# Hybrid decoder trunk on one core: ScalarE reads a bank ahead of VectorE, and keys and B are turned by VectorE and DRAM

## The chip, the cores and the metric

One core of a Trainium2 chip runs the whole kernel as one program. The metric is device time in microseconds, median of the runs.

## What is computed

Two layers over 512 positions of width 1024. Each layer norms the residual, projects it once to all heads (w_in), feeds four groups of heads, gates each group, projects back (w_out), norms and adds.

```python
hn = rmsnorm(x, pre_g)
proj = hn @ w_in
...
# retention, per head of 128, chunks of 128
q = apply_rope(q)
k = apply_rope(k) * (d ** -0.5)
scores = jnp.einsum('bcnhd,bcmhd->bchnm', qc, kc) * intra.astype(dt)
y_intra = jnp.einsum('bchnm,bcmhe->bcnhe', scores, vc)
kv = jnp.einsum('bcmhd,bcmhe->bchde', kc * zeta.astype(dt)[:, :, None], vc)
...
# state space (SSD), two groups of B and C, chunks of 128
cb = jnp.einsum('bclgn,bcsgn->bclsg', cc, bc)
states = jnp.einsum('bclgn,bclgjp->bcgjpn', bc, xdt * decay_states.astype(dtype)[..., None])
...
# stick-breaking, per block of 128 queries
logits = jnp.einsum('bthd,bshd->bhts', q_blk, k).astype(jnp.float32) * scale
log_1mb = jnp.where(causal, jax.nn.log_sigmoid(-logits), 0.0)
tail = lax.cumsum(log_1mb, axis=3, reverse=True) - log_1mb
w = jnp.where(causal, jnp.exp(log_beta + tail), 0.0)
...
y = jnp.concatenate([y_ret, y_ssd, y_sb, y_mem], axis=-1) @ w_out
return x + rmsnorm(y, post_g)
```

The fourth group (mem) is softmax attention over 256 fixed memory tokens, four heads of 128.

## The kernel before

**Pairs.** fp32 products are made of rounded halves. A `Pair` holds a high half h (rounded) and a low half l = x − h, and `mm3` makes three matmuls of two pairs. `split` (L289 to L291) makes a pair: ScalarE rounds into h (L290), VectorE subtracts for l (L291). Weights arrive by DMA as raw tiles and are split the same way into wh and wl. A projection of 128 output features is a block of 24 matmuls of 128x512 on a PSUM bank called pj; the heads' own products go to banks called mx. There are four banks of each, and a bank is free again when its last reader is done.

**Order of the work.** `layer` runs: stick-breaking's v, four memory heads, four stick-breaking heads, retention's v, four retention heads each followed by a gated memory block, two state-space groups with the gated stick-breaking blocks between, four gated retention blocks, and the output projection. `defer(n, f, ...)` puts the second part of a head n projection blocks later, so that its products are issued among the projections of the next heads. Within that, a scheduler orders the instructions of each engine by its own times, so an edit in one place moves instructions of other places too. Every engine and every DMA queue then works in the order that it was given: SP's queue carries the turned tiles and the decay loads, ScalarE's the raw weights.

**What the change touches.**

- `scaled_pair` (L582 to L586) and `first_chunk` (L588 to L591) serve `sb_head` (L687 to L722). A head's q and k each sit in a pj bank. For q ScalarE writes h, scaled (L584), VectorE l (L585), and ScalarE reads the bank once more for an fp32 copy of the first 128 columns (L590). For k it is `split` and then L590. The four score blocks, of 128, 256, 384 and 512 columns, go through Abs (L709), exponential and logarithm (both L259) on ScalarE, L712, the scan L713 and L715 on VectorE, and a last exponential; L718 masks on GpSimd. Later they are turned by TensorE (L729).
- `ret_head` (L795 to L817): q and k are rotated by VectorE (L769 to L772), the scores of two pairs of chunks go into one mx bank each, which `split` (L805) and a copy (L806) read before GpSimd masks (L808). The first two chunks of k are turned by TensorE (L811) and copied out by ScalarE (L812) into kt; `ret_state`, two blocks later, multiplies kt with v.
- `mem_turn` (L626 to L633): VectorE turns 32 by 32 blocks (L641), four 64 KB writes per tile put them in place in DRAM (L649), and one read brings them back (L651). L663 empties a memory head's bank.
- `ssd_mix` (L986 to L998): the first three chunks of B are turned by TensorE (L996) and copied by ScalarE (L997); `ssd_states` uses them. L959 loads the decays of a group's heads from DRAM, L961 subtracts on VectorE, L962 masks, and L976 turns x on TensorE.

The lines of ret_head that the change rewrites:

```python
kt, b = f[:, 2 * P:], self.mx()
for c in range(2):
    nc.tensor.transpose(b[:, P * c:P * c + P], k.f[:, P * c:P * c + P], self.con("ident", P))
nc.scalar.copy(kt, b[:, :2 * P])
st = self.new(2 * P, F32R)
self.defer(2, self.ret_state, h, v, kt, st)
```

Of the kernel before, what the change touches and what calls it, by code (L numbers as in the profile page):

```python
# [8 lines left out]
F32 = mybir.dt.float32  # L9
# [7 lines left out]
P = 128  # L17
# [136 lines left out]

ROW = 128


# [12 lines left out]
class Builder:  # L172
# [406 lines left out]
            self.mv.append(p)  # L579


    def scaled_pair(self, b, scale):  # L582
        q = Pair(self)
        self.nc.scalar.activation(q.h, b, AF.Copy, scale=scale)  # L584
        self.nc.vector.scalar_tensor_tensor(out=q.l, in0=b, scalar=scale, in1=q.hf, op0=ALU.mult, op1=ALU.subtract)  # L585
        return q  # L586

    def first_chunk(self, b, scale, out):  # L588

        self.nc.scalar.activation(out, b[:, :P], AF.Copy, scale=scale)  # L590
        return out  # L591

    @staticmethod
    def vcols(v, t, h):
# [29 lines left out]
        return o  # L624

    def mem_turn(self, h, w, y):  # L626
        pT = []
        for m in range(2):
            T = self.buf(tag="y")
            for t in range(NT):  # L630
                o = 256 * (t % 2) + P * m
                self.blocks_turned(T, t, w[t // 2][:, o:o + P])
            pT.append(self.through_dram(T))  # L633
        self.defer(4, self.mem_head2, h, pT, y)

    def blocks_turned(self, T, t, x):


        B = 32
        n = T.shape[1] // P  # L640
        self.nc.vector.transpose(v3(T, P // B)[:, :, B * t:B * t + B], v3(x, P // B))  # L641

    def through_dram(self, T, tag="s"):

        B = 32
        d = self.dr.tile([P, SEQ], F32, tag="turned", name=self.name("turned"), bufs=4)[:]
        dd = d.rearrange("(j m) (a t) -> a m j t", m=B, a=P // B)
        for a in range(P // B):
            self.nc.sync.dma_start(dd[a], v3(T[B * a:B * a + B], P // B))  # L649
        x = self.buf(tag="y")  # L650
        self.nc.sync.dma_start(x, d)  # L651
        return x

    def mem_head2(self, h, pT, y):
        pT = [self.pair(x) for x in pT]
# [31 lines left out]
    def sb_head(self, h, v):  # L687
        nc = self.nc
        f = self.buf(3 * P)
        b = self.proj_b()  # L690
        q = self.scaled_pair(b, SCALE)
        q.f = self.first_chunk(b, SCALE, f[:, :P])
        b = self.proj_b()
        k = self.pair(b)
        k.f = self.first_chunk(b, 1.0, f[:, P:2 * P])
        w = [t[:, c] for t, c in self.packed([P * (t + 1) for t in range(NT)], self.buf)]
        run = self.con("run", SEQ)
        for t in range(NT):
# [96 lines left out]
    def ret_head(self, h, v):  # L795
        nc = self.nc
        q = self.rope(self.proj_b())
        k = self.rope(self.proj_b())
        sc, f = Pair(self), self.buf()
        for i in range(2):  # L800
            b, o, fs = self.mx(), 2 * P * i, slice(P * i, P * i + P)
            c, last = slice(o, o + 2 * P), slice(o + P, o + 2 * P)
            self.mm3(b[:, :2 * P], k.h[:, o:o + P], k.l[:, o:o + P], q.h[:, c], q.l[:, c], True, True)
            self.mm(b[:, 2 * P:3 * P], k.f[:, last], q.f[:, last], True, True)
            self.split(b[:, :2 * P], sc.h[:, c], sc.l[:, c], sc.hf[:, c])  # L805
            nc.scalar.copy(f[:, fs], b[:, 2 * P:3 * P])  # L806
            for d in (sc.h[:, o:o + P], sc.l[:, o:o + P], f[:, fs]):
                nc.gpsimd.affine_select(out=d, in_=d, pattern=[[1, P]], compare_op=ALU.is_ge, fill=0.0, base=0, channel_multiplier=-1)  # L808
        kt, b = f[:, 2 * P:], self.mx()
        for c in range(2):  # L810
            nc.tensor.transpose(b[:, P * c:P * c + P], k.f[:, P * c:P * c + P], self.con("ident", P))  # L811
        nc.scalar.copy(kt, b[:, :2 * P])  # L812
        st = self.new(2 * P, F32R)
        self.defer(2, self.ret_state, h, v, kt, st)
        y = self.buf(tag="y")
        self.defer(4, self.ret_head2, h, v, sc, f, st, q, y)
        return y  # L817
# [116 lines left out]
    def ssd_group(self, l, g, ysb):  # L934

        X = {"l": l, "g": g}
        self.ssd_decay(X)
        X["x"] = [self.conv(self.proj_b(), 2 * g + i) for i in range(2)]
        self.defer(2, self.ssd_values, X)
        self.gated(("sb", 2 * g), ysb[2 * g])  # L940
        X["b"] = self.conv(self.proj_b(), 4 + g)
        X["c"] = self.conv(self.proj_b(), 6 + g)
        self.defer(3, self.ssd_mix, X)
        self.gated(("sb", 2 * g + 1), ysb[2 * g + 1])
        X["y"] = [self.buf(tag="y"), self.buf(tag="y")]
        X["z"] = [self.gate(self.proj_b()) for _ in range(2)]
        self.defer(1, self.ssd_states, X)
        self.defer(3, self.ssd_out, X, 0)
        self.defer(3, self.ssd_out, X, 1)
        self.defer(5, self.ssd_var, X)  # L950
        self.defer(9, self.ssd_norm, X)
# [34 lines left out]
    def ssd_mix(self, X):  # L986
# [4 lines left out]
            self.mm(cb[:, s], bT[:, s], cT[:, s], True, True)  # L991
        for a in X["A"]:
            nc.vector.tensor_tensor(out=a, in0=a, in1=cb, op=ALU.mult)
        bt, b = self.buf(), self.mx()
        for c in range(NT - 1):
            nc.tensor.transpose(b[:, P * c:P * c + P], bT[:, P * c:P * c + P], self.con("ident", P))  # L996
        nc.scalar.copy(bt[:, :384], b[:, :384])  # L997
        X["bt"] = bt  # L998

    def ssd_states(self, X):  # L1000

# [311 lines left out]
```

## Time and profile before

| | |
|---|---|
| median of 3 runs | 939.14 us (938.91 to 940.09) |
| profiled execution | 938.47 us |
| its span, first to last instruction | 936.7 us |
| mean granted TensorE clock | 0.998 |
| matmul instructions (PE) | 4775 |
| busy: PE, PEld, DVE, ACT, POOL | 99%, 84%, 71%, 48%, 11% |

PE is TensorE, PEld its weight load, DVE VectorE, ACT ScalarE, POOL GpSimd, SP the queue that issues most transfers. A timeline row gives start, duration, engine, line, operation, output<-input, how many instructions of the kind stand in a row, and in brackets the idle time before them with what ended it. Times count from the start of the span.

### The profile page before, as it was taken

The page shows a single profiled execution, that of the slowest core. Times are in us where ns is not written, and L with a number is a line of the kernel's source. Part 1 is how long each engine was busy: PE and PEld are TensorE (multiplying, and loading weights), DVE is VectorE, ACT ScalarE, POOL GpSimd, SP SyncE. Part 2 cuts the span into 40 slices and gives each one's busy share as a digit, 9 for nine tenths or more (in the row PEclk, how much of TensorE's full clock was granted, in tenths as well). Part 3 has the DMA queues.
Part 4 walks back from the last instruction along what each step waited for, and adds up shares of the span by engine and source line. Part 5 has one row for each costly group of instructions (what it writes and reads, how often), then busy time and mean ns, then how long its engine had stood idle before and what let it go on. Part 6 is the DMA issues. An engine that isn't in the chain of part 4 may idle for free.

```text
span 936.7 us, 12791 instructions
## 1 busy us (share of the span) xinstructions
PE 925.5 (99%) x4775; PEld 784.3 (84%) x4775; DVE 667.3 (71%) x1109; ACT 451.6 (48%) x861; POOL 103.3 (11%) x168
## 2 busy tenths in 40 slices
PE   9999999999999999999999999999999999999997
PEld 8998878888888888888899887888888888888885
DVE  6946687767778886844587467878676989687343
ACT  7733585643354442733465337665343644336341
POOL 1200011100031110100050000101000411102001
PEclk9999999999999999999999999999999999999999
DMA  9544530412423423344345265112223252323502
GB/s 325 209 152 125 182 117 1 135 45 91 135 67 136 136 91 124 135 146 157 118 177 181 92 185 174 46 46 90 90 91 135 69 175 96 124 73 105 205 12 90
DMA packets 38910, 114.35 MB, mean 122 GB/s; under 512 B 5824, under 2 KB 14272, under 8 KB 29760
## 3 DMA queue, kind: packets, MB, share of 16 engines
q10 hardware_dynamic: 10224, 73.44, 22.6%
q1 hardware_dynamic: 28624, 40.11, 13.4%
q8 instruction: 37, 0.61, 0.3%
q14 instruction: 25, 0.20, 0.1%
HBM read 105.02 MB, written 8.48 MB: 121 GB/s over the span
## 4 chain that ended last, share of the span: by engine, by line
PE 96%; ACT 1%; DVE 1%; DMA 0%; issue 0%; DVEq 0%; SPq 0%; ACTq 0%; POOLq 0%; POOL 0%
PE pj L282 72%; PE mx L282 22%; PE mx L729 1%; PE mx L476 1%; DMA mem<-memT 0%; DVE s L713 0%; PE mx L976 0%; ACT s L709 0%; ACT wh L290 0%; DVE s L291 0%; PE mx L811 0%; DVE s L712 0%; DVE s L585 0%; ACT s L520 0%; PE mx L996 0%
## 5 line engine op out<-in xcount | busy, mean ns | idle before, releaser
L282 PE MATMUL pj<-hTh,wh 128*128 128x512 f32 x704 | 277.7, 394 | 2.5 <-ACT s L590 2.5
L291 DVE TENSOR_TENSOR wl<-raw,wh 128x1024 fp32r<-128x1024 f32 (+2 forms) x156 | 184.6, 1187 | 130.5 <-ACT wh L290 129.7
L282 PE MATMUL pj<-hTh,wl 128*128 128x512 f32 x704 | 275.6, 392 | 0.0
L282 PE MATMUL pj<-hTl,wh 128*128 128x512 f32 x704 | 275.1, 391 | 0.0
L290 ACT CAST wh<-raw 128x1024 fp32r<-128x1024 f32 (+2 forms) x156 | 158.6, 1020 | 229.5 <-PE pj L282 208.2
L282 PEld LDWEIGHTS pj<-hTh,wh 128*128 128x128 f32 x704 | 132.3, 188 | 30.3 <-ACT s L590 3.3
L282 PEld LDWEIGHTS pj<-hTh,wl 128*128 128x128 f32 x704 | 132.3, 188 | 27.1
L282 PEld LDWEIGHTS pj<-hTl,wh 128*128 128x128 f32 x704 | 132.3, 188 | 26.3
L282 PE MATMUL pj<-wh,s 128*128 128x512 f32 x320 | 97.7, 391 | 0.0
L282 PE MATMUL mx<-wh,s 128*128 128x512 f32 x256 | 79.2, 389 | 0.0
L282 PE MATMUL mx<-s,s 128*128 128x256 f32 (+3 forms) x528 | 77.7, 307 | 0.0
L291 DVE TENSOR_TENSOR s<-y,s 128x512 fp32r<-128x512 f32 x80 | 51.9, 684 | 27.5 <-ACT s L290 21.8
L282 PEld LDWEIGHTS mx<-s,s 128*128 128x128 f32 (+1 forms) x528 | 65.4, 177 | 7.2 <-issue 2.3
L282 PEld LDWEIGHTS pj<-wh,s 128*128 128x128 f32 x320 | 59.7, 188 | 12.4
L290 ACT CAST s<-y 128x512 fp32r<-128x512 f32 x80 | 46.5, 618 | 28.6 <-PE mx L282 22.0
L282 PE MATMUL pj<-wl,s 128*128 128x512 f32 x160 | 60.2, 389 | 0.0
L282 PEld LDWEIGHTS mx<-wh,s 128*128 128x128 f32 x256 | 48.1, 188 | 10.0
L259 ACT ACTIVATE s<-s 128x384 f32<-128x384 f32 (+3 forms) x96 | 41.4, 479 | 20.8 <-DVE s L715 20.7
L282 PE MATMUL mx<-wl,s 128*128 128x512 f32 x128 | 49.6, 389 | 0.0
L718 POOL TENSOR_SCALAR_AFFINE_SELECT s<-s 128x128 f32<-128x128 f32 x32 | 17.8, 565 | 280.5 <-ACT s L259 280.5
L282 PE MATMUL pj<-wl,hTh 128*128 128x256 f32 (+2 forms) x144 | 48.1, 334 | 0.0
L282 PE MATMUL pj<-wh,hTl 128*128 128x256 f32 (+2 forms) x144 | 48.0, 334 | 0.0
(185 smaller groups left out, 1273.0 us busy)
## 6 DMA issues: line engine op xcount, KB each, us to landing
raw<-wts ACTq DMA_DIRECT2D x69, 1024.0 KB, 4.8
s<-x SPq DMA_DIRECT2D x24, 256.0 KB, 3.8
turned<-y SPq DMA_DIRECT2D x64, 64.0 KB, 2.3
y<-turned SPq DMA_DIRECT2D x16, 256.0 KB, 2.8
s<-acs SPq DMA_DIRECT2D x16, 256.0 KB, 7.2
r<-row SPq DMA_DIRECT2D x12, 256.0 KB, 4.1
raw<-wts SPq DMA_DIRECT2D x4, 512.0 KB, 6.6
raw<-wts SPq DMA_DIRECT2D x2, 1024.0 KB, 6.4
```

The source lines that it names most:

```text
L259: i = self.nc.scalar.activation(out, in_, func, **k)
L282: return self.nc.tensor.matmul(out, lhsT, rhs, start=start, stop=stop)
L290: self.nc.scalar.copy(h, src)
L291: self.nc.vector.tensor_sub(l, src, hf)
L476: x = self.nc.tensor.transpose(b[:, P * j:P * j + P], hn[i][:, P * j:P * j + P], self.con("ident", P))
L718: nc.gpsimd.affine_select(out=d, in_=d, pattern=[[-1, P]], compare_op=ALU.is_gt, fill=0.0, base=0, channel_multiplier=1)
L729: nc.tensor.transpose(b[:, P * t:P * t + P], w[t][:, P * j:P * j + P], self.con("ident", P))
```

## The change

- `scaled_pair` makes the high half, then ScalarE's first-chunk copy, then VectorE's low half, for q and now for k too (scale 1.0, a subtraction). `first_chunk` is gone.
- In `ret_head` ScalarE copies the high half of the scores and the fp32 chunk, and VectorE subtracts last.
- The first two chunks of a retention head's keys, and the first three of B, are turned by `columns_turned`: one VectorE transpose of 32 by 32 blocks, four writes to DRAM in runs of 128 bytes, and one read back. `ret_state` comes four blocks later rather than two. B's turn is issued at B's convolution, and its buffer taken there.
- `mem_turn` turns 256 columns with one instruction, with the same DRAM traffic.

```diff
-    def scaled_pair(self, b, scale):
+    def scaled_pair(self, b, scale, f):
         q = Pair(self)
         self.nc.scalar.activation(q.h, b, AF.Copy, scale=scale)
-        self.nc.vector.scalar_tensor_tensor(out=q.l, in0=b, scalar=scale, in1=q.hf, op0=ALU.mult, op1=ALU.subtract)
+        self.nc.scalar.activation(f, b[:, :P], AF.Copy, scale=scale)
+        if scale == 1.0:
+            self.nc.vector.tensor_sub(q.l, b, q.hf)
+        else:
+            self.nc.vector.scalar_tensor_tensor(out=q.l, in0=b, scalar=scale, in1=q.hf, op0=ALU.mult, op1=ALU.subtract)
+        q.f = f
         return q
...
     def mem_turn(self, h, w, y):
...
-            for t in range(NT):
-                o = 256 * (t % 2) + P * m
-                self.blocks_turned(T, t, w[t // 2][:, o:o + P])
-            pT.append(self.through_dram(T))
+            for i in range(2):
+                x = w[i].rearrange("p (t m j b) -> p m t j b", t=2, m=2, b=BLK)[:, m]
+                nc.vector.transpose(T.rearrange("p (j t b) -> p t j b", t=NT, b=BLK)[:, 2 * i:2 * i + 2], x)
+            d = self.turned_rows(P, SEQ)
+            dd = d.rearrange("(j m) (a t) -> a m j t", m=BLK, a=P // BLK)
+            pT.append(self.through_dram(T, dd, d, self.buf(tag="y")))
...
+    def columns_turned(self, tiles, out):
+        n = sum(x.shape[1] for x in tiles[:1])
+        d = self.turned_rows(n, P * len(tiles))
+        for k, x in enumerate(tiles):
+            T = self.buf(n, TT)
+            self.nc.vector.transpose(T, x)
+            dd = d[:, P * k:P * k + P].rearrange("(b t) (a f) -> a t b f", t=BLK, a=P // BLK)
+            for a in range(P // BLK):
+                self.nc.sync.dma_start(dd[a], v3(T[BLK * a:BLK * a + BLK], n // BLK))
+        r = d.rearrange("(c p) f -> p c f", p=P)
+        c = 0
+        for o in out:
+            k = o.shape[1] // (P * len(tiles))
+            self.nc.sync.dma_start(v3(o, k), r[:, c:c + k])
+            c += k
...
     def sb_head(self, h, v):
...
-        q = self.scaled_pair(b, SCALE)
-        q.f = self.first_chunk(b, SCALE, f[:, :P])
+        q = self.scaled_pair(b, SCALE, f[:, :P])
         b = self.proj_b()
-        k = self.pair(b)
-        k.f = self.first_chunk(b, 1.0, f[:, P:2 * P])
+        k = self.scaled_pair(b, 1.0, f[:, P:2 * P])
...
     def ret_head(self, h, v):
...
-            self.split(b[:, :2 * P], sc.h[:, c], sc.l[:, c], sc.hf[:, c])
+            nc.scalar.copy(sc.h[:, c], b[:, :2 * P])
             nc.scalar.copy(f[:, fs], b[:, 2 * P:3 * P])
+            nc.vector.tensor_sub(sc.l[:, c], b[:, :2 * P], sc.hf[:, c])
...
-        kt, b = f[:, 2 * P:], self.mx()
-        for c in range(2):
-            nc.tensor.transpose(b[:, P * c:P * c + P], k.f[:, P * c:P * c + P], self.con("ident", P))
-        nc.scalar.copy(kt, b[:, :2 * P])
+        kt = f[:, 2 * P:]
+        self.columns_turned([k.f[:, :2 * P]], [kt])
         st = self.new(2 * P, F32R)
-        self.defer(2, self.ret_state, h, v, kt, st)
+        self.defer(4, self.ret_state, h, v, kt, st)
...
         X["b"] = self.conv(self.proj_b(), 4 + g)
+        X["bt"] = self.buf()[:, :3 * P]
+        self.columns_turned([X["b"][:, :3 * P]], [X["bt"]])
         X["c"] = self.conv(self.proj_b(), 6 + g)
...
-        bt, b = self.buf(), self.mx()
-        for c in range(NT - 1):
-            nc.tensor.transpose(b[:, P * c:P * c + P], bT[:, P * c:P * c + P], self.con("ident", P))
-        nc.scalar.copy(bt[:, :384], b[:, :384])
-        X["bt"] = bt
```

Over the program this takes 28 transposes off TensorE (16 of L811, 12 of L996) and 12 copies off ScalarE, and adds 60 transfers on SP (48 writes, 12 reads). VectorE's transposes go from 64 to 44.

Three places show how instructions move; the names end in running numbers, and pj, mx, s, y, wh, wl are the tiles told of above.

VectorE in layer 1, from a split of a turned memory tile (y178) to the low half of head 1's q in bank pj246; s233 holds the 128 and 256 wide score blocks of head 0, s234 the 384, s235 the 512. Before:

```order
L291 TENSOR_TENSOR s243_1335<-y178_1010,s242_1334 128x512
L712 SCALAR_TENSOR_TENSOR s233_1283<-mx236_1286,s233_1283 128x128
L712 SCALAR_TENSOR_TENSOR s233_1283<-mx237_1296,s233_1283 128x256
L713 SCALAR_TENSOR_TENSOR s233_1283<-consts_72,s233_1283 128x128
L713 SCALAR_TENSOR_TENSOR s233_1283<-consts_72,s233_1283 128x256
L712 SCALAR_TENSOR_TENSOR s234_1284<-mx238_1308,s234_1284 128x384
L715 TENSOR_TENSOR s233_1283<-mx236_1286,s233_1283 128x128
L715 TENSOR_TENSOR s233_1283<-mx237_1296,s233_1283 128x256
L291 TENSOR_TENSOR s245_1339<-y181_1022,s244_1338 128x512
L713 SCALAR_TENSOR_TENSOR s234_1284<-consts_72,s234_1284 128x384
L712 SCALAR_TENSOR_TENSOR s235_1285<-mx239_1320,s235_1285 128x512
L585 SCALAR_TENSOR_TENSOR s251_1374<-pj246_1342,s250_1373 128x512
```

and now:

```order
L726 SCALAR_TENSOR_TENSOR s233_1267<-mx236_1270,s233_1267 128x128
L727 SCALAR_TENSOR_TENSOR s233_1267<-consts_72,s233_1267 128x128
L729 TENSOR_TENSOR s233_1267<-mx236_1270,s233_1267 128x128
L293 TENSOR_TENSOR s243_1319<-y178_1000,s242_1318 128x512
L726 SCALAR_TENSOR_TENSOR s233_1267<-mx237_1280,s233_1267 128x256
L727 SCALAR_TENSOR_TENSOR s233_1267<-consts_72,s233_1267 128x256
L729 TENSOR_TENSOR s233_1267<-mx237_1280,s233_1267 128x256
L293 TENSOR_TENSOR s245_1323<-y181_1010,s244_1322 128x512
L726 SCALAR_TENSOR_TENSOR s234_1268<-mx238_1292,s234_1268 128x384
L726 SCALAR_TENSOR_TENSOR s235_1269<-mx239_1304,s235_1269 128x512
L727 SCALAR_TENSOR_TENSOR s234_1268<-consts_72,s234_1268 128x384
L592 SCALAR_TENSOR_TENSOR s251_1358<-pj246_1326,s250_1357 128x512
```

The same eleven operations stand ahead of the low half of q; the narrowest block's three now come ahead of the split of y178.

TensorE in layer 1, where stick-breaking's last head meets retention's v (pj338); L729 and now L743 turn the weights of head 0. Before:

```order
L729 MATMUL mx288_1537<-consts_72,s235_1285 128x128
L729 MATMUL mx289_1544<-consts_72,s233_1283 128x128
L729 MATMUL mx289_1544<-consts_72,s234_1284 128x128
L729 MATMUL mx289_1544<-consts_72,s235_1285 128x128
L282 MATMUL pj338_1818<-wh258_1419,hTh_79 128x512
```

and now, where the "..." stands for 18 more matmuls of pj338:

```order
L743 MATMUL mx288_1521<-consts_72,s235_1269 128x128
L284 MATMUL pj338_1802<-wh258_1403,hTh_79 128x512
...
L284 MATMUL pj338_1802<-wl310_1669,hTh_79 128x512
L743 MATMUL mx289_1528<-consts_72,s233_1267 128x128
L743 MATMUL mx289_1528<-consts_72,s234_1268 128x128
```

The turns into bank mx289 moved behind 20 matmuls of the retention projection.

SP in layer 1, at the end of retention: the decay loads of the first state-space group. Before, they follow the memory heads' last turned tile:

```order
L649 DMA turned216_1198<-y215_1193 32x4x128 x4
L651 DMA y217_1203<-turned216_1198 128x512
L959 DMA s514_2737<-acs134_722 128x512
L959 DMA s515_2744<-acs134_722 128x512
```

and now they follow the turned keys of retention's heads 2 and 3:

```order
L662 DMA turned468_2480<-y469_2481 32x8x32 x4
L667 DMA s465_2457<-turned468_2480 128x2x128
L662 DMA turned500_2654<-y501_2655 32x8x32 x4
L667 DMA s497_2631<-turned500_2654 128x2x128
L974 DMA s518_2737<-acs134_722 128x512
L974 DMA s519_2744<-acs134_722 128x512
```

Four writes and a read per retention head now stand ahead of the decay loads.

## Rows read from the trace of the kernel before

**Rows 1.** The page, busy times by engine and DMA packets.

```profile
PE 925.5 (99%) x4775; PEld 784.3 (84%) x4775; DVE 667.3 (71%) x1109; ACT 451.6 (48%) x861; POOL 103.3 (11%) x168
...
DMA packets 38910, 114.35 MB, mean 122 GB/s; under 512 B 5824, under 2 KB 14272, under 8 KB 29760
```

**Rows 2.** The page, chain that ended last, by engine.

```profile
PE 96%; ACT 1%; DVE 1%; DMA 0%; issue 0%; DVEq 0%; SPq 0%; ACTq 0%; POOLq 0%; POOL 0%
```

**Rows 3.** TensorE's waits: line waited for, us in total, times, longest.

```profile
PE pj L282 <- ACT s L590: 2.5, 2, 1.2
...
PE mx L729 <- ACT y L663: 0.7, 2, 0.3
```

**Rows 4.** Groups by line: count | busy us, mean ns | idle before.

```profile
L641 DVE STREAM_TRANSPOSE y<-s 128x128 f32<-128x128 f32 x64 | 14.4, 278 | 0.0
...
L811 PE MATMUL mx<-consts,s 128*128 128x128 f32 x16 | 3.0, 272 | 0.0
...
L996 PE MATMUL mx<-consts,s 128*128 128x128 f32 x12 | 2.0, 273 | 0.0
```

**Rows 5.** The chain in order of time: start, us, what, two pieces.

```profile
306.00 0.33 PE mx L996 x3
...
386.23 40.13 PE pj L282 x177
```

**Rows 6.** Timeline 114 to 126 us, ScalarE, VectorE and TensorE.

```profile
115.10 0.93 ACT L709 ACTIVATE s<-mx 128x128 f32<-128x128 f32 x3
115.91 0.63 ACT L259 ACTIVATE s<-s 128x128 f32<-128x128 f32 x2
...
117.97 0.69 DVE L291 TENSOR_TENSOR s<-y,s 128x512 fp32r<-128x512 f32 x1 [1.51 <-ACT s L290]
...
120.31 0.61 ACT L584 ACTIVATE s<-pj 128x512 fp32r<-128x512 f32 x1
...
123.16 0.67 DVE L585 SCALAR_TENSOR_TENSOR s<-pj,s 128x512 fp32r<-128x512 f32 x1
...
124.19 0.50 PE L282 MATMUL pj<-hTh,wh 128*128 128x512 f32 x1 [1.23 <-ACT s L590]
```

**Rows 7.** Timeline 137 to 141 us, TensorE and VectorE.

```profile
138.43 0.60 PE L729 MATMUL mx<-consts,s 128*128 128x128 f32 x4
...
138.78 0.67 DVE L585 SCALAR_TENSOR_TENSOR s<-pj,s 128x512 fp32r<-128x512 f32 x1
...
139.36 0.52 PE L729 MATMUL mx<-consts,s 128*128 128x128 f32 x3 [0.33 <-ACT y L663]
...
139.81 0.19 PEld L282 LDWEIGHTS pj<-wh,hTh 128*128 128x128 f32 x1 [0.18 <-ACT s L590]
```

**Rows 8.** Timeline 240 to 275 us, SP, VectorE and TensorE.

```profile
245.52 1.99 SPq L959 DMA_DIRECT2D s<-acs  x4
...
258.37 0.69 DVE L772 TENSOR_TENSOR s<-s,s 128x512 f32<-128x512 f32 x1
...
265.03 0.38 PE L811 MATMUL mx<-consts,s 128*128 128x128 f32 x2
...
273.01 1.01 DVE L961 TENSOR_TENSOR s<-s,t 128x512 f32<-128x512 f32 x1
```

**Rows 9.** Timeline 111 to 116 us, SP's issues for a turned memory tile.

```profile
111.85 1.77 SPq L649 DMA_DIRECT2D turned<-y  x4
...
115.06 0.34 SPq L651 DMA_DIRECT2D y<-turned  x1
```

**Rows 10.** DMA issues: count, KB each, median us from issue to landing.

```profile
turned<-y SPq DMA_DIRECT2D x64, 64.0 KB, 2.3
y<-turned SPq DMA_DIRECT2D x16, 256.0 KB, 2.8
s<-acs SPq DMA_DIRECT2D x16, 256.0 KB, 7.2
...
t<-r SPq DMA_DIRECT2D x12, 2.0 KB, 1.7
```

More of the change, by code (lines that the diff above doesn't have):

```diff
@@ L153, in shape_constants @@
     return c
+BLK = 32
+TT = "y"
 ROW = 128
@@ L579, in mem_v2 @@
             self.mv.append(p)
-    def scaled_pair(self, b, scale):
+    def scaled_pair(self, b, scale, f):
         q = Pair(self)
         self.nc.scalar.activation(q.h, b, AF.Copy, scale=scale)
-        self.nc.vector.scalar_tensor_tensor(out=q.l, in0=b, scalar=scale, in1=q.hf, op0=ALU.mult, op1=ALU.subtract)
-        return q
-    def first_chunk(self, b, scale, out):
-        self.nc.scalar.activation(out, b[:, :P], AF.Copy, scale=scale)
-        return out
+        self.nc.scalar.activation(f, b[:, :P], AF.Copy, scale=scale)
[4 more added lines that the diff above has]
+        q.f = f
+        return q
     @staticmethod
@@ L626, in mem_turn @@
     def mem_turn(self, h, w, y):
+        nc = self.nc
         pT = []
@@ L629, in mem_turn @@
             T = self.buf(tag="y")
-            for t in range(NT):
-                o = 256 * (t % 2) + P * m
-                self.blocks_turned(T, t, w[t // 2][:, o:o + P])
-            pT.append(self.through_dram(T))
-        self.defer(4, self.mem_head2, h, pT, y)
[L636 to L652, printed above, removed]
+            for i in range(2):
+                x = w[i].rearrange("p (t m j b) -> p m t j b", t=2, m=2, b=BLK)[:, m]
+                nc.vector.transpose(T.rearrange("p (j t b) -> p t j b", t=NT, b=BLK)[:, 2 * i:2 * i + 2], x)
@@ new lines, in mem_turn, with turned_rows, through_dram @@
+            d = self.turned_rows(P, SEQ)
+            dd = d.rearrange("(j m) (a t) -> a m j t", m=BLK, a=P // BLK)
+            pT.append(self.through_dram(T, dd, d, self.buf(tag="y")))
+        self.defer(4, self.mem_head2, h, pT, y)
+    def turned_rows(self, n, m):
+        return self.dr.tile([n, m], F32, tag=f"turned{n}", name=self.name("turned"), bufs=4)[:]
+    def through_dram(self, T, dst, src, out):
+        n = dst.shape[2]
+        for a in range(P // BLK):
+            self.nc.sync.dma_start(dst[a], v3(T[BLK * a:BLK * a + BLK], n))
+        self.nc.sync.dma_start(out, src)
+        return out
@@ new lines, in columns_turned @@
+    def columns_turned(self, tiles, out):
[5 more added lines that the diff above has]
+            dd = d[:, P * k:P * k + P].rearrange("(b t) (a f) -> a t b f", t=BLK, a=P // BLK)
+            for a in range(P // BLK):
+                self.nc.sync.dma_start(dd[a], v3(T[BLK * a:BLK * a + BLK], n // BLK))
[5 more added lines that the diff above has]
+            c += k
```

## The prediction

> **What bounds the kernel.** I began with the page's busy times: TensorE is busy for 925.5 of 936.7 us, VectorE for 71%, ScalarE for 48% [rows 1]. The chain that ended last says the same from the other side: 96% of it is TensorE [rows 2]. So an edit can gain in two ways only: it takes a matmul off TensorE, or it closes a gap in front of one. The granted clock was 0.998, the 2.4 GHz level, over the whole span, so nothing is to be won or lost there.
>
> For the gaps I read TensorE's waits [rows 3]. There are four kinds in all, and the two that matter stand there: line 590 (2.5 us, 2 times, one per layer) and line 663 (0.7 us, 2 times); the change bears on both. The other two, on GpSimd's line 194 and ScalarE's line 520, belong to parts that it leaves alone. Last I read the timeline around both gaps in layer 1 [rows 6, 7]; layer 2 repeats them 460 us later. The sum is made against the profiled execution, 938.47 us; the median of the runs shown is 939.14, that is 0.67 more, and I add that at the end.
>
> **Turns taken off TensorE.** The 16 transposes of line 811 and the 12 of line 996 go [rows 4]. The page's 272 ns is the length of one, not its price, since matmuls overlap. The price is the pitch, which the chain in order of time shows: three of line 996 take 0.33 us there [rows 5], 0.11 us each, and line 811's have the same form. So 28 cost 3.08 us. These stand on the path with no gap in front of them; this term is the safest. The eight copies of line 812 and four of line 997 on ScalarE go as well; TensorE waits for neither, so I count nothing for them.
>
> The row shows a turn at 0.11 us, on an engine that has no free time. The Trainium skill, VectorE: DVE Perf Modes, section Rules for kernel authors, recommends TensorE for a 128 by 128 transpose where PSUM will do as its destination, because VectorE turns 32 by 32 blocks only. By that rule the 28 would be better left, and the sum would lose its first term; the row and the 99% speak against it here.
>
> **What VectorE takes over.** Eight turns of 128x256 and four of 128x384 come, and the memory heads' 64 turns of 128x128 become 32 of twice the size. One of the old takes 278 ns [rows 4]; a new one of 256 columns lies between 0.28 us (only a fixed cost) and 0.56 us (in proportion), one of 384 between 0.28 and 0.83. I take the proportion: at most 7.8 us more on VectorE, less what the memory heads save, on an engine with 269 us idle. The key turn is put ahead of the key's low half, for which the scores wait; TensorE's waits name no half of a key, so the half has some cover there, and I cost half a microsecond at nothing. If that cover were gone, the scores would start half a microsecond late, eight times.
>
> **The turned keys' way through DRAM.** Four writes and a read per head, on SP. The nearest rows are the memory heads' own: from the first of four writes issued to the read issued 3.21 us (111.85 to 115.06) [rows 9], the read lands 2.8 us later [rows 10], so 6.0 us. The new writes carry half the bytes in runs of 128 bytes, 256 runs each. I bound their landing by 1.7 us (the 2 KB writes t<-r, the smallest there) and twice the old 2.3, 4.6 us [rows 10], so the trip by 5.4 and 8.3 us. Head 3's keys are complete at 259.06 [rows 8]; its scores are done when line 811 starts, at 265.03 [rows 8], and the order puts some 8 us of projection between them and the state product, at about 273. That is 13.9 us for a trip of 6; the other heads have a whole head's period, 20 us. Cost: nothing. B of the state space has two projection blocks of 5.4 us more before its use, and costs nothing either.
>
> **The gap on line 590.** In the old order ScalarE rounds q at 120.31, VectorE makes its low part at 123.16, and only then does ScalarE copy the first chunk; until that has read the bank, head 3's q can't start, and TensorE idles 1.23 us [rows 6]. Its last product would have let it start at 124.19 − 1.23 = 122.96. In the new order the copy follows the rounding at once, so ScalarE is out by about 121.3, and VectorE's low part releases the bank. When does it end? The same eleven operations stand ahead of it since the weights' low half, but the order is another: the 128-wide block's three come first, ahead of the split of y. In the old run VectorE idled 1.51 us before that split, to 117.97 [rows 6]. The block's logarithm is now ScalarE's sixth operation after the weight cast, ready near 116.8 (three Abs and two exponentials end at 115.91 + 0.63 = 116.54 [rows 6], a logarithm like one of these adds 0.3). So about 1.0 us of VectorE's work moves into that gap and the low part ends near 123.83 − 1.0 = 122.8 (the eleven took 123.16 − 117.97 = 5.19 us, under half a microsecond each; the three of the narrowest block come to about 1.0). Bounds: if nothing fits, it ends at 123.83 and 0.87 us of the gap stay; at best none does. I take 0.08 left, the end that the order of the rows is nearest to: 1.15 gained, twice, **2.3 us**.
>
> **The gap on line 663.** At 139.36 three transposes wait 0.33 us for a PSUM bank that line 663 empties; then the first retention block waits another 0.18 us for line 590 [rows 7]. In the new order 20 matmuls of that block (4.5 us at 0.227 [rows 5]) stand ahead of the three transposes, so the wait on line 663 is covered. The block itself then wants VectorE's low part at 138.43 + 0.44 = 138.87; it ended at 138.78 + 0.67 = 139.45 [rows 7], and an order changed in the same way brings it 1.0 forward, to about 138.5. Bounds: none to 0.55 gained per layer (0.33 + 0.18, and the first matmul's longer 0.50). I take 0.45, twice: **0.9 us**.
>
> The retention scores' new order (both copies on ScalarE, then the subtraction) has one waiter that the order shows, GpSimd's masking; TensorE's waits name neither. I cost it at nothing.
>
> **Sum:** 3.08 + 2.3 + 0.9 = 6.28. 938.47 − 6.28 = 932.19; with 0.67, **932.9 us**.
>
> **Rivals.**
> 1. The gaps change hands only. The eleven operations could end as late as before, VectorE's low part then holding the bank where ScalarE's copy did. For it: all eleven are still there, and both gaps lie at one engine's pace. Against it: the 1.51 us hole [rows 6]. With 0.87 left twice and nothing gained at the second gap, 3.08 + 0.72 = 3.8 are gained: 935.3; with both gaps as they were, 936.1.
> 2. SP's queue takes it back. SP works in order, and the decay loads of line 959, issued at 245.52 [rows 8], now stand behind head 3's key read, which waits for four writes. They can't go before about 262.5; the four take 2 us to issue and the median lands 7.2 us after its issue [rows 8, 10], so the last lands at about 272 by the old times, where VectorE wants it at 273.01 [rows 8]. Late by 0 to 2 us if they land slower than that median, VectorE then makes the state space's convolution late, for whose transposes TensorE waits with some 0.8 us in hand. Price 0 to 2 us per layer, so up to 4: 934 to 936.9.
> 3. The other side: the key's trip is long. If head 3's trip takes more than the 13.9 us in hand, TensorE stops in front of its state product, with gated projections queued behind it. The gain is eaten at (6.28 + 1.9) / 2 = 4.1 us beyond, a trip of 18 us, and the time is then over 941. That needs the writes to land 12 us later than the old ones; for it speaks that 14,336 packets of 128 bytes are added to 38,910, against it that the smallest writes landed in 1.7 us [rows 1, 10]. The Trainium skill, DMA: Bandwidth & Descriptors, section Specifications, has transfers reach full rate from 512 bytes only; by that rule the 128-byte runs are where this case would come from, and no row here shows them in such a number.
>
> **Chances.** A difference of 0.2%, 1.9 us, is about what a measurement can tell here. The forecast (both gaps mostly closed, no new wait over a microsecond) 0.55; the first rival 0.17; the second 0.20; the third 0.03; and 0.05 for a wait on another engine that no row points to, half of it past 941. The first rival and 0.14 of the second stay under 937.3; in the other 0.06 the decay loads take longer than their median all four, and the time falls within 0.2%. So faster has 0.86, within 0.2% 0.08, slower 0.06. Low end: every gap closed gives 3.08, the 2.5 + 0.7 of the waits [rows 3] and twice the 0.18 at 139.81 [rows 7], 6.6; with a run at the lower edge (0.23 under the median) that is 932.3, and I leave 1.1 below it for the matmuls that run long after a gap (0.50 for 0.39 [rows 6]) and for stops shorter than the view names: 931.2. High end: the second rival's worst, 936.9.
>
> **What would show it.** No row of lines 811 or 996 on TensorE, and 28 fewer matmuls; line 590's or 592's wait under 0.3 us each; no wait on line 663's successor before the first retention block; the first-chunk copy directly behind the rounding on ScalarE. The key writes landing within 5 us. It is wrong if the profile shows a VectorE low part ending later than 123.3 in head 1, a wait of TensorE on the key read, or a new wait in front of the state space's transposes.

## The result, and the profile after

The changed kernel takes 933.95 us (median of 6 runs, 932.8 to 935.38) where the kernel before took 939.29 (median of 6, 938.91 to 940.09): the ratio is 0.9941, with a 95% interval of 0.993 to 0.9952. Its profiled execution took 932.86 us with a span of 931.1, 5.6 us under the span before. One run each of three kernels below had a granted clock of 0.75 or 0.85 and took 1021 to 1157 us; the ratios leave these runs out, and the medians move by 0.2 us at most without them.

TensorE's busy time and the chain of the changed kernel, from its page:

```profile
PE 922.4 (99%) x4747; PEld 781.7 (84%) x4747; DVE 672.1 (72%) x1089; ACT 444.0 (48%) x849; POOL 92.2 (10%) x168
...
PE 94%; DVE 2%; ACT 2%; DMA 1%; issue 0%; DVEq 0%; SPq 0%; ACTq 0%; POOLq 0%; POOL 0%
```

Against [rows 1] 28 matmuls and 3.1 us of TensorE are gone, and VectorE has 4.8 us more. TensorE's waits in the changed kernel:

```profile
PE mx L284 <- POOL b L196: 1.2, 1, 1.2
PE pj L284 <- DVE s L592: 1.0, 2, 0.5
PE pj L284 <- ACT s L522: 0.3, 1, 0.3
```

Against [rows 3], the wait on line 663 is gone. The one on line 590 has changed hands and is less than half: where ScalarE's copy released the bank after 1.2 us, VectorE's low half now does after 0.5. The timeline of the changed kernel around this place, VectorE, ScalarE and TensorE, answers to [rows 6]:

```profile
117.03 0.29 DVE L726 SCALAR_TENSOR_TENSOR s<-mx,s 128x128 f32<-128x128 f32 x1 [0.41 <-ACT s L261]
...
118.03 0.69 DVE L293 TENSOR_TENSOR s<-y,s 128x512 fp32r<-128x512 f32 x1
118.76 0.42 DVE L726 SCALAR_TENSOR_TENSOR s<-mx,s 128x256 f32<-128x256 f32 x1
...
119.22 0.69 DVE L727 TENSOR_TENSOR_SCAN s<-consts,s 128x256 f32<-128x256 f32 x1
...
119.94 0.42 DVE L729 TENSOR_TENSOR s<-mx,s 128x256 f32<-128x256 f32 x1
120.28 0.68 DVE L293 TENSOR_TENSOR s<-y,s 128x512 fp32r<-128x512 f32 x1
...
121.27 0.28 ACT L588 ACTIVATE s<-pj 128x128 f32<-128x128 f32 x1
...
122.95 0.66 DVE L592 SCALAR_TENSOR_TENSOR s<-pj,s 128x512 fp32r<-128x512 f32 x1
...
123.66 0.50 PE L284 MATMUL pj<-hTh,wh 128*128 128x512 f32 x1 [0.52 <-DVE s L592]
```

ScalarE has left the bank at 121.55 (forecast: 121.3); the low half ends at 123.61, 0.8 later than forecast, of which 0.18 is this run's later start. At the second place the low half ends at 138.50, and the first retention block starts right behind it, with no wait for the memory bank ahead of it; compare [rows 7]:

```profile
137.84 0.66 DVE L592 SCALAR_TENSOR_TENSOR s<-pj,s 128x512 fp32r<-128x512 f32 x1
137.87 0.60 PE L743 MATMUL mx<-consts,s 128*128 128x128 f32 x4
...
138.55 0.50 PE L284 MATMUL pj<-wh,hTh 128*128 128x512 f32 x1
```

SP's issues for head 3's keys and the decay loads behind them, against [rows 8, 9]:

```profile
251.98 1.79 SPq L662 DMA_DIRECT2D turned<-y  x4
255.73 0.38 SPq L667 DMA_DIRECT2D s<-turned  x1
256.21 1.83 SPq L974 DMA_DIRECT2D s<-acs  x4
```

The first write was issued at 251.98 and the read landed at 257.87, 5.9 us later; the other three trips of the layer took 7.1, 5.0 and 7.7 us, those of layer 2 5.3, 5.2, 8.4 and 6.0, and B's four 6.7 to 7.8. No wait of TensorE names a key or B.

**How the profiles are compared.** The first 22 us of a run, where the inputs arrive, differ by over 3 us from one execution to the next (last section). So where a profile is set against another below, the time counts from TensorE's first turn of the normed input (line 476 before, 478 after, some 22 us into the span) to the end of the span: 936.74 − 22.18 = 914.56 before, 931.14 − 22.36 = 908.78 after, 5.78 less.

### The profile page after: what moved, and what is told of

The parts are those of the page before. It is cut to its first block, busy times and chain, and to the rows that moved or that the text cites. A ratio compares the mean times of both kernels' runs of the same rounds, so it can differ in the third digit from the quotient of the medians.

```text
span 931.1 us, 12813 instructions
## 1 busy us (share of the span) xinstructions
PE 922.4 (99%) x4747; PEld 781.7 (84%) x4747; DVE 672.1 (72%) x1089; ACT 444.0 (48%) x849; POOL 92.2 (10%) x168
## 2 busy tenths in 40 slices
DMA packets 57790, 118.03 MB, mean 127 GB/s; under 512 B 21120, under 2 KB 33152, under 8 KB 48640
## 4 chain that ended last, share of the span: by engine, by line
PE 94%; DVE 2%; ACT 2%; DMA 1%; issue 0%; DVEq 0%; SPq 0%; ACTq 0%; POOLq 0%; POOL 0%
PE pj L284 71%; PE mx L284 21%; PE mx L743 1%; PE mx L478 1%; DVE s L727 1%; DVE s L726 1%; ACT wh L292 1%; DMA mem<-memT 1%; ACT s L261 0%; PE mx L991 0%; ACT s L723 0%; DVE s L293 0%; DVE wl L293 0%; DVE s L592 0%; ACT s L292 0%
## 5 line engine op out<-in xcount | busy, mean ns | idle before, releaser
L284 PE MATMUL mx<-s,s 128*128 128x256 f32 (+4 forms) x528 | 81.1, 307 | 0.0
L261 ACT ACTIVATE s<-s 128x128 f32<-128x128 f32 (+3 forms) x96 | 41.3, 471 | 23.3 <-DVE s L729 23.1
L284 PE MATMUL pj<-wh,hTh 128*128 128x256 f32 (+2 forms) x144 | 48.3, 336 | 0.2
```

Of the source, the lines that this page charges most:

```text
L261: i = self.nc.scalar.activation(out, in_, func, **k)
L284: return self.nc.tensor.matmul(out, lhsT, rhs, start=start, stop=stop)
```

## The experiments

**The two halves of the change, alone.** First the changed kernel once more.

> The changed kernel once more, beside the others of this call. Theory (28 turns at 0.109 us off TensorE, and gaps in front of TensorE that shrank from 4.5 to 2.3 us): about 933.9, 5.3 under the kernel before. Rival (SP's longer queue and the small writes give some of it back, by an amount that varies from run to run): the same median, with runs that spread over 2 us or more where the kernel before spreads over 1.2, and a profile of a slower run that shows a wait for a DMA which the first profile does not have.

It took 934.0 us, ratio 0.9939 (0.9925 to 0.9952), the same as the first time. The four runs that the ratio uses lie within 0.7 us of each other, where the rival had a spread over 2; the six of the result lie within 2.6, so the spread itself is not settled. Whether SP's queue takes a part is left to the last run of this section.

Then the order of reads alone (`scaled_pair` with its calls, and the scores), all turns as before:

```diff
-        q = self.scaled_pair(b, SCALE)
-        q.f = self.first_chunk(b, SCALE, f[:, :P])
+        q = self.scaled_pair(b, SCALE, f[:, :P])
...
             nc.scalar.copy(f[:, fs], b[:, 2 * P:3 * P])
+            nc.vector.tensor_sub(sc.l[:, c], b[:, :2 * P], sc.hf[:, c])
```

> Only the order of reads: q, k and retention scores read by ScalarE first, by VectorE last; all turns as before. Theory: the gaps alone shrink, 2 x (1.50 - 0.79) + 2 x (0.72 - 0.35) = 2.2 us: about 937.1. Rival (the order of reads gives nothing by itself, the gaps shrank because the turns left VectorE and ScalarE in another order): 939.3, with waits on the low half of q of 1.2 us each.

Measured: 936.91 us, ratio 0.9975 (0.9966 to 0.9985); 912.11 us from the first turn, 2.45 less than before. TensorE waits 0.3 us at line 592 twice. The theory holds, and the size.

The other half, the turns of keys, B and memory weights, with all reads as before:

```diff
+        self.columns_turned([k.f[:, :2 * P]], [kt])
...
-        self.defer(2, self.ret_state, h, v, kt, st)
+        self.defer(4, self.ret_state, h, v, kt, st)
...
-                self.blocks_turned(T, t, w[t // 2][:, o:o + P])
+                nc.vector.transpose(T.rearrange("p (j t b) -> p t j b", t=NT, b=BLK)[:, 2 * i:2 * i + 2], x)
```

> Only the turns: retention keys, B and the memory weights as in the change; q, k and scores read as before. Theory: 28 x 0.109 = 3.05 us off TensorE and nothing given back, and both gaps of the kernel before stay (line 590's successor 1.2 us twice): about 936.2. Rival (the trip through DRAM or VectorE's added turns cost TensorE something): 937 or more, with a new wait in TensorE's list.

Measured: 937.0 us, ratio 0.9975 (0.9965 to 0.9985); 912.21 from the first turn, 2.35 less and not 3.05. Of the 2.35, 0.33 lie behind the last matmul (told below at keys and B alone), so TensorE's part is 2.02, 1.0 short of the theory. A new wait stands in TensorE's list, as the rival had it, but not on a transfer:

```profile
PE pj L284 <- ACT s L592: 1.9, 2, 1.0
PE mx L284 <- DVE s L730: 1.3, 2, 0.7
...
PE mx L744 <- ACT y L678: 0.7, 2, 0.3
```

It is VectorE's last step of a score block in stick-breaking, a part that the turns don't touch. So the order of instructions there is what to look at for the missing 1.0 us; the next run settles it. The two halves gain 4.8 us alone and 5.78 together: 1.0 us hangs on their meeting.

**Which turn costs it.** Memory weights alone:

```diff
-            for t in range(NT):
-                o = 256 * (t % 2) + P * m
-                self.blocks_turned(T, t, w[t // 2][:, o:o + P])
+            for i in range(2):
+                x = w[i].rearrange("p (t m j b) -> p m t j b", t=2, m=2, b=BLK)[:, m]
+                nc.vector.transpose(T.rearrange("p (j t b) -> p t j b", t=NT, b=BLK)[:, 2 * i:2 * i + 2], x)
```

> Only the memory weights' turn in half as many instructions of 256 columns; all else as in the kernel before. Theory (in the run with the turns alone it was this edit that put VectorE's three 128, 256 and 384 wide blocks side by side, and that made the gaps at the first two heads 2.15 us where they were 1.50): no matmul goes and the gaps grow by 0.65 twice: about 940.8. Rival (the edit moves nothing that counts, and the trip through DRAM of keys and B made those gaps): 939.4.

Measured: 940.9 us, as forecast, ratio 1.0012 (1.0004 to 1.0021); 915.85 from the first turn, 1.29 more than before, with the same wait on line 730 (1.3 us, 2 times) as in the run with all turns. VectorE's timeline of this run:

```profile
119.60 1.08 DVE L727 SCALAR_TENSOR_TENSOR s<-mx,s 128x128 f32<-128x128 f32 x3
120.60 1.85 DVE L728 TENSOR_TENSOR_SCAN s<-consts,s 128x128 f32<-128x128 f32 x3
122.36 0.67 DVE L293 TENSOR_TENSOR s<-y,s 128x512 fp32r<-128x512 f32 x1
```

Three blocks of 128, 256 and 384 columns go through each step side by side, and the split of y starts at 122.36 behind all three scans. Behind it comes the last step of the narrowest block, line 730, for which TensorE's next product waits: TensorE stops for 0.66 us until 123.29, and for 0.95 until 125.89. Fewer instructions on VectorE made this kernel slower, through the order that the scheduler made of the rest.

Keys and B alone, memory weights and reads as before:

```diff
+        self.columns_turned([k.f[:, :2 * P]], [kt])
...
-        self.defer(2, self.ret_state, h, v, kt, st)
+        self.defer(4, self.ret_state, h, v, kt, st)
...
+        X["bt"] = self.buf()[:, :3 * P]
+        self.columns_turned([X["b"][:, :3 * P]], [X["bt"]])
```

> Only keys and B turned by VectorE and DRAM; memory weights and all reads as in the kernel before. Theory: VectorE's order in stick-breaking stays as it was before, both gaps keep their 4.47 us, and 28 x 0.109 us go: about 936.4. Rival (the trip through DRAM costs about half a microsecond, which is what the run with all turns fell short of 3.05): 937 or more, with a wait of TensorE on a key, on B or on the decays.

Measured: 936.05 us, ratio 0.9961 (0.9949 to 0.9974); 911.16 from the first turn, 3.40 less. 0.32 of that lies behind the last matmul (6.73 us from its start to the end before, 6.42 here and 6.41 in the changed kernel), so 3.08 are TensorE's, against 3.05 forecast. The waits on lines 590 and 663 are back at 2.5 and 0.7. The rival falls: the trip through DRAM costs TensorE nothing, and no wait of TensorE in this run names a key, B or the decays.

Retention scores alone:

```diff
-            self.split(b[:, :2 * P], sc.h[:, c], sc.l[:, c], sc.hf[:, c])
+            nc.scalar.copy(sc.h[:, c], b[:, :2 * P])
             nc.scalar.copy(f[:, fs], b[:, 2 * P:3 * P])
+            nc.vector.tensor_sub(sc.l[:, c], b[:, :2 * P], sc.hf[:, c])
```

> Only the retention scores' order of reads (both ScalarE copies first, VectorE's subtraction last); all else as in the kernel before. Theory (TensorE waits for none of these reads): the same as before, 939.3, within 0.5. Rival (part of the 2.5 us that the order of reads gained came from here): 938.5 or less.

Measured: 939.12 us, ratio 0.9998 (0.9988 to 1.0008); 914.57 from the first turn. Nothing, as forecast.

**What is left of the gaps.** If VectorE's low half, behind eleven operations, now holds the bank, then a kernel in which ScalarE alone reads it has no gap:

```diff
+    def wide_pair(self, b, scale):
+        q, x = Pair(self), self.buf()
+        self.nc.scalar.activation(q.h, b, AF.Copy, scale=scale)
+        self.nc.scalar.activation(x, b, AF.Copy, scale=scale)
+        self.nc.vector.tensor_sub(q.l, x, q.hf)
+        q.f = x[:, :P]
+        return q
...
-        q = self.scaled_pair(b, SCALE, f[:, :P])
+        q = self.wide_pair(b, SCALE)
```

> The change, with q's fp32 copy 512 columns wide instead of 128, so that VectorE makes the low half from SBUF and ScalarE alone frees the bank. Theory (what is left of the gaps, 0.79 + 0.35 us per layer, is VectorE's low half behind eleven other operations): both gaps close, 2.3 us less than the change: about 931.6. Rival (ScalarE's longer copy delays exponentials and heads by as much, or something else stands ready behind VectorE): 933 to 935, with a wait of the same places on ScalarE.

Measured: 930.9 us, ratio to the kernel before 0.9912 (0.9899 to 0.9926), 3.1 under the change; 906.60 from the first turn, 2.18 under it. ScalarE's rows and TensorE's at the same place of this run:

```profile
120.98 0.61 ACT L600 ACTIVATE s<-pj 128x512 f32<-128x512 f32 x1
...
122.53 0.71 DVE L601 TENSOR_TENSOR s<-s,s 128x512 fp32r<-128x512 f32 x1
...
122.69 0.39 PE L284 MATMUL pj<-hTh,wh 128*128 128x512 f32 x1
```

VectorE's low half starts at 122.53, counted from the first turn 0.1 us earlier than in the change, and ends at 123.24; TensorE starts at 122.69 without a wait. That the low half's place held the bank in the change is thereby shown. The 0.33 us longer copy on ScalarE costs nothing.

**The key's trip and SP's queue.** The change with the turned keys sent through DRAM once more:

```diff
-        self.columns_turned([k.f[:, :2 * P]], [kt])
+        way = self.buf(2 * P, TT)
+        self.columns_turned([k.f[:, :2 * P]], [way])
+        d = self.dr.tile([P, 2 * P], F32, tag="again", name=self.name("again"), bufs=4)[:]
+        nc.sync.dma_start(d, way)
+        nc.sync.dma_start(kt, d)
```

> The change, with the turned keys sent through DRAM a second time, a plain write of 128 KB and a read back, so that SP carries 16 transfers more and a key is late by one more round trip of about 5 us. Theory (13.9 us in hand for head 3 and 20 for the others, 6 used): no change, 933.9. Rival (SP's queue is what the change has used up: decay loads behind the key read come late, and the state space's transposes wait): 935 or more, with a wait of TensorE on VectorE or on a transfer near 270 us.

Measured: 936.06 us, ratio 0.9959 (0.9947 to 0.9972), 2 us over the change: the theory's number is missed. The five runs reach from 934.36 to 937.09, and the profiled one is the slowest. From the first turn it is 3.3 us over the change, in two places of layer 1. About 1.6 of these go at 44 us, ahead of every key, where TensorE waits for a weight that came late:

```profile
44.61 0.51 PE L284 MATMUL pj<-wh,hTh 128*128 128x256 f32 x2 [1.36 <-ACT wh L292]
```

The other 1.7 are the second trip's. TensorE waits for no key. It waits for the state space's sums at 319 us, and VectorE's timeline of this run shows why:

```profile
310.90 0.69 DVE L980 TENSOR_TENSOR s<-s,t 128x512 f32<-128x512 f32 x1 [4.11 <-DMA s<-acs]
311.51 2.47 DVE L1012 TENSOR_TENSOR s<-s,mx 128x512 f32<-128x512 f32 x4
```

The first decay of the second group (L980) now stands ahead of four products of the first (L1012); in the change the four come first. VectorE works in order, so it waited 4.11 us for a load with ready work behind it. The kernel that took the decay loads off SP tells which it was:

```diff
-            nc.sync.dma_start(v3(a, 4), S["rows"][0, r:r + 4].unsqueeze(0).to_broadcast([P, 4, P]))
+            nc.gpsimd.dma_start(v3(a, 4), S["rows"][0, r:r + 4].unsqueeze(0).to_broadcast([P, 4, P]))
...
-            nc.sync.dma_start(v3(E[64 * j:64 * j + 64], 4), S["rows"][1, r:r + 4].unsqueeze(0).to_broadcast([64, 4, P]))
+            nc.gpsimd.dma_start(v3(E[64 * j:64 * j + 64], 4), S["rows"][1, r:r + 4].unsqueeze(0).to_broadcast([64, 4, P]))
```

> The run with the keys' second trip, decay loads issued from GpSimd's queue in place of SP's. Theory (a key later by a whole round trip harms nothing; what the second trip cost was VectorE standing 4.1 us in front of the second group's decays with four ready products of the first group queued behind it): those loads and their subtractions go back behind the products, and the time is that of the change, 933.9, within 0.7. Rival (the key's longer trip itself is what costs): 935.5 or more, with TensorE waiting for a key or its state product.

Measured: 933.71 us, ratio 0.9939 (0.9925 to 0.9952), the change's time, with 908.88 from the first turn against its 908.78. Neither of the two waits is there. A key that comes a whole round trip later (head 3's last read landed at 265.02, 13.6 us after the first write) harms nothing.

**More of the same.** The wide copy, with the state space's x turned by VectorE and DRAM too:

```diff
+        X["xt"] = [self.buf(), self.buf()]
+        self.columns_turned(X["x"], X["xt"])
-        self.defer(2, self.ssd_values, X)
+        self.defer(3, self.ssd_values, X)
...
-                    nc.tensor.transpose(b[:, o:o + P], X["x"][j][:, P * c:P * c + P], self.con("ident", P))
+            b = X["xt"][i]
```

> The run with the wide copy of q, and besides the state space's x turned by VectorE and DRAM too, 32 transposes of TensorE less, one projection block later. Theory (a turn off TensorE is worth its pitch wherever the trip has cover): 32 x 0.109 = 3.5 us under the wide copy's 930.9: about 927.4. Rival (VectorE or SP has no room in the state space, where four decay loads, B and the row norms are already queued): 930 or more, with a new wait of TensorE on VectorE's products of x.

Measured: 945.83 us, ratio 1.0067 (1.0053 to 1.008), slower than the kernel before. VectorE waited for decays that stood in SP's queue behind x's turned reads, and TensorE then waited for VectorE (VectorE's row and TensorE's):

```profile
336.80 0.55 DVE L1049 TENSOR_TENSOR s<-s,mx 128x384 f32<-128x384 f32 x1 [5.50 <-DMA s<-acs]
```

```profile
352.64 0.39 PE L284 MATMUL mx<-r,onesr 128*1 128x512 f32 x1 [2.30 <-DVE r L1062]
356.33 0.77 PE L284 MATMUL pj<-hTh,wh 128*128 128x512 f32 x1 [3.30 <-DVE s L937]
356.89 0.63 PE L284 MATMUL pj<-hTl,wh 128*128 128x512 f32 x1
357.32 0.63 PE L284 MATMUL pj<-hTh,wl 128*128 128x512 f32 x1
```

The same, with the decay loads moved to GpSimd's queue by the edit shown above:

> The run that turned x too, with one edit: the decay loads are issued from GpSimd's queue in place of SP's. Theory (x turned on VectorE lost 15 us because the loads stood in SP's queue behind the turned reads of x, and VectorE waited 5.5 us for them): the two gaps of 3.8 and 1.2 us in front of TensorE go and the 32 x 0.109 us are gained: 927 to 930. Rival (VectorE has no room in the state space for x's turns, whatever the queue): 940 or more, with VectorE's convolution and norm products still named by TensorE's waits.

Measured: 929.23 us, ratio 0.9893 (0.9877 to 0.991), the fastest kernel of this study, 4.7 us under the change and 10 under the kernel before; 904.51 from the first turn, 2.1 under the wide copy, with no wait of TensorE behind the first 10 us. The time lies within the theory's 927 to 930, but the 3.5 us of 32 pitches are not reached: 2.1 us are 0.07 for a turn of x, where a turn of keys and B gave 0.11. Why is open. The wide copy with the loads moved alone:

> The run with the wide copy of q, decay loads issued from GpSimd's queue in place of SP's. Theory (at the state space's second group VectorE waits about 1.4 us for these loads, but TensorE has cover for it): the same as the wide copy, 930.9, within 0.5. Rival (SP's queue still costs the change something): 930 or less.

Measured: 931.62 us, ratio 0.9918 (0.9903 to 0.9933); 906.69 from the first turn against 906.60. The median is 0.7 over that of the wide copy, more than the 0.5 of the theory, but in the profiles that lies ahead of the first turn. Moving the loads gains nothing by itself, so SP's queue costs the wide copy nothing (the change itself was not run so); it is what stops the next step.

## Why the prediction was right, and where it was off

The forecast was 932.9 us, the measured median 933.95. 6.28 us were to go; 5.34 went by the medians, and 5.78 by the profiles from the first turn on, which is what the terms below are set against. That the profiled run, 932.86 us, meets the forecast is luck: it is the second fastest of six.

- **Turns off TensorE, 3.08.** Right: keys and B alone gave 3.08 us of TensorE's time. The pitch of 0.11 us was the price of a turn here, and the 0.272 of the group's row would have been wrong by 4.5 us. Agreement to the last digit is luck: the profiles of the wide copy with and without the loads moved differ by 0.09 us.
- **The gap on line 590, 2.3.** The mechanism was right and its size off: 2 × (1.23 − 0.52) = 1.4 by the waits. The step that failed is "the eleven took 5.19 us": they were given that time in another order too, and took 122.95 − 117.03 = 5.92. The kernel before, VectorE:

```profile
118.58 0.61 DVE L712 SCALAR_TENSOR_TENSOR s<-mx,s 128x128 f32<-128x128 f32 x2
119.11 1.00 DVE L713 TENSOR_TENSOR_SCAN s<-consts,s 128x128 f32<-128x128 f32 x2
120.03 0.53 DVE L712 SCALAR_TENSOR_TENSOR s<-mx,s 128x384 f32<-128x384 f32 x1
120.48 0.61 DVE L715 TENSOR_TENSOR s<-mx,s 128x128 f32<-128x128 f32 x2
121.01 0.68 DVE L291 TENSOR_TENSOR s<-y,s 128x512 fp32r<-128x512 f32 x1
```

  Here equal steps of the 128 and the 256 wide block stand side by side, and a row starts some 0.08 us before the one ahead ends. The six steps take 0.53 + 0.92 + 0.53 = 1.98 us from start to start. In the changed kernel the three steps of one block follow each other, and each starts only when the one ahead, whose result it reads, is done (118.76 + 0.42 = 119.18, and 119.22). The six take 1.00 (117.03 to 118.03) and 1.52 (118.76 to 120.28), 0.54 more, of the 0.73 by which the eleven are longer. Counted from the first turn VectorE began 1.1 us earlier, as forecast, but its low half ended only 0.4 earlier. By two of the prediction's own signs this term was wrong: the low half ended behind 123.3 in head 1, and the wait was 0.5 where under 0.3 was said.
- **The gap on line 663, 0.9.** The wait for the memory bank went as forecast. The first retention block starts at 138.55, 0.24 us behind the last transpose (137.87 + 0.44 = 138.31), for the low half, so by the waits 2 × (0.33 + 0.18 − 0.24) = 0.5 were gained. The waits miss a part. Here is a product that both kernels reach behind the same number of matmuls, before and after:

```profile
148.24 0.39 PE L282 MATMUL pj<-wh,hTh 128*128 128x512 f32 x1
```

```profile
147.31 0.39 PE L284 MATMUL pj<-wh,hTh 128*128 128x512 f32 x1
```

  Counted from the first turn it stands at 126.06 before and at 124.95 now, 1.11 earlier. 0.71 of that was there at the first gap (102.01 and 101.30), so the second place gave 0.40; layer 2 repeats it (1.09 for both places). That is 0.8 in all, and this term was nearly right.
- **The sum.** 1.4 and 0.8 for the gaps, 3.2 for the rest of TensorE's span, in which the 28 turns went, and the 0.32 us behind the last matmul (below) make 5.8, which is what the profiles differ by. So the first gap's 2.3 is the term that was too large, by 0.9, and 0.32 came from a place that the forecast did not look at.
- **Costs put at nothing.** The scores (no change in the run with them alone), the trip of the keys and the copies (keys and B alone gave all of their 3.08) were rightly at nothing. Of the eight trips of a key, 5.0 to 8.4 us where 6.0 was said, four lie within the bounds of 5.4 to 8.3, three are shorter and one is 0.1 longer; a second trip harmed nothing. A VectorE turn of 256 columns takes 0.40 to 0.45 us and one of 384 takes 0.58, between the bounds. The memory weights' turn was put at nothing too and is not: alone it costs 1.3 us. In the change it costs next to nothing: keys and B (3.40) and the order of reads (2.45) alone make 5.85, and all together make 5.78.
- **The rivals.** The first (gaps change hands) is what happened to half of the gaps. From the first turn the wide copy, which closes both, gained 2.2 us more, as much as the change had gained at them, and that TensorE then started ahead of the low half's end showed who held the bank. The second (SP's queue) did not happen in the change: head 3's keys were complete at 251.47, where the kernel before had them at 259.06, so the decay loads went out at 256.21 and not at 262.5, and moving them off SP gained nothing in the wide copy. But its mechanism is real: with more transfers on SP it cost 1.7 us in one profile and then 15, at the second group's decays and not at the first's. The third needed a trip of 18 us; with 13.6 nothing waited.

The 0.32 us behind the last matmul, of which all kernels with keys and B turned through DRAM gained 0.2 to 0.33, lies in how the program closes. In both kernels the last output write lands about as late behind that matmul's start (5.64 us before, 5.57 now). SP then passes five waits that close the program: before, all five come behind that landing, and in the changed kernel only one does. Why the scheduler puts a decay ahead of ready products when SP's queue is longer was not followed up; it is seen in the run with the second trip, and its cause is not in these profiles.

## What to carry to other kernels

Price a matmul that goes by its pitch on the path as a first estimate (28 turns gave it in full, x's 32 gave two thirds of it), and an operation that stays by who holds the bank last: the low half held its bank until VectorE had come to it behind eleven others, so let the engine with the shorter queue read the bank, even for a longer copy. An operation that depends on the one ahead starts later than one that doesn't (here 0.04 us behind its end and not 0.08 before it), so a sum of durations taken from one order does not hold in another. An edit that takes instructions off an engine can still lose through the order that a scheduler makes of the rest; compare the order at the known gaps before counting it as free. And a load in an in-order queue is late when something ahead of it waits, so what others wait for belongs on a queue of its own before more transfers are added.

## What was not expected of the hardware

- **The first 22 us vary.** TensorE's first turn started between 22.08 and 25.25 us in thirteen profiles, before and after among them. In the run with the order of reads alone TensorE waited 2.08 us for the memory's first rounded tile, where the run before waited 0.21:

```profile
9.06 0.51 PE L284 MATMUL pj<-s,wh 128*128 128x256 f32 x2 [2.08 <-ACT s L522]
```

  The granted clock of the following stretch, from 10 to 16 us, was 0.72 in that run and 1.00 in the kernel before. A start like that is worth more than the difference between two of these kernels, so profiles are better compared from behind it. Even that does not catch everything: in the run with the keys' second trip a weight was late at 44 us, for 1.36.

- **A stop costs more than its length.** In the run with x turned and the loads on SP, TensorE was busy for 0.73 of the 6 us from 350 to 356, and then ran at the lower level for some 6 us. The busy times by stretch of that run, the last three numbers of a row being the granted clock, the DMA share and GB/s:

```profile
350.00:356.00 6.00, 0.73 (x3) 0.08 (x1) 5.90 (x12) 2.48 (x4) 0.46 (x2) 0.95 0.54 198
356.00:360.00 4.00, 3.67 (x9) 2.96 (x10) 3.24 (x6) 2.09 (x4) 2.65 (x1) 0.50 0.02 5
360.00:364.00 4.00, 4.00 (x15) 3.19 (x14) 0.03 (x1) 0.00 (x0) 0.00 (x0) 0.72 0.36 115
```

  At 0.50, the 1.2 GHz level, the matmuls stand 0.43 us apart (356.89, 357.32), where they stand 0.23 apart at 2.4 GHz. The waits on VectorE sum to 11.2 us over that run; from the first turn it took 921.25 us, 14.7 over the wide copy. The 32 turns less were worth 2.1 us once the loads had moved, so some 5.6 us are the clock's and other losses. The gaps of the kernel before, at most 1.23 us, left the clock alone.

- **Small writes landed quickly.** Each write of a key moves 32 KB in pieces of 128 bytes and landed a median of 1.7 us after its issue, against 2.0 for the memory weights' 64 KB in pieces of 512. Each of B's, 48 KB in pieces of 128 bytes, took 3.5:

```profile
turned<-y SPq DMA_DIRECT2D x64, 64.0 KB, 2.0
...
turned<-y SPq DMA_DIRECT2D x32, 32.0 KB, 1.7
...
turned<-y SPq DMA_DIRECT2D x16, 48.0 KB, 3.5
```

  For the keys, half the bytes in twice the packets took no longer. B's 3.5 us are not the price of its pieces alone: in the run with x turned and the loads on SP, B's four writes from 291.12 us landed 1.6 to 1.8 us after their issue. What slows them in the changed kernel was not followed up. By the rule of the Trainium skill on small transfers that the prediction named (DMA: Bandwidth & Descriptors, section Specifications), the pieces of 128 bytes would run below full rate; that may be so, but no wait of TensorE showed it.
